# Attention stream of a trunk layer: layer norms written in four steps, the first output rows loaded one block sooner, the value products of a group in one run

## The chip, the core and the metric

The kernel runs on one core of a Trainium2 chip. The core has five engines with a queue of their own each, which run their instructions in the order of the queue: PE (TensorE, matrix products; PEld is its weight load), DVE (VectorE), ACT (ScalarE), POOL (GpSimd) and SP (SyncE, which here issues the DMA transfers). The metric is the time of one execution on the device in microseconds (us), the median of several runs.

## What is computed

One decoder layer on 2048 rows of 1024 numbers: stick-breaking attention with 12 heads of 64, cross-attention of 4 heads into 256 memory rows, an output projection, a layer norm, a squared-ReLU MLP of width 4096 and a second layer norm. The part around the change:

```python
def stick_breaking_attention(q, k, v):
    for blk in range(seq // SB_BLOCK):
        z = jnp.einsum('bhtd,bhsd->bhts', qb, kb).astype(jnp.float32) * scale
        strict = jnp.arange(t1)[None, :] < jnp.arange(t0, t1)[:, None]
        log_stay = jnp.where(strict, jax.nn.log_sigmoid(-z), 0.0)
        later = lax.cumsum(log_stay, axis=3, reverse=True) - log_stay
        w = jnp.where(strict, jnp.exp(jax.nn.log_sigmoid(z) + later), 0.0)
        outs.append(jnp.einsum('bhts,bhsd->bhtd', w.astype(vb.dtype), vb))
...
y = jnp.concatenate([mix, mem_out.astype(mix.dtype)], axis=-1) @ w_out[layer]
x = layer_norm(DN_ALPHA * x + y, ln_mix_g[layer], ln_mix_b[layer])
h = jnp.square(jax.nn.relu(x @ w_up[layer]))
x = layer_norm(DN_ALPHA * x + h @ w_down[layer], ln_ffn_g[layer], ln_ffn_b[layer])
```

## The kernel before

**Numbers.** Products run in fp16 with each operand split into a high and a low half, so a product is three passes (`PASSES`). ACT makes a high half, DVE or POOL the low one (`split_ps`, L161 and L162).

**Stages.** A first stage transposes x, projects the first pair of heads and does the memory heads (to about 236 us of the span). Then `attention` writes one long stream for the six pairs of heads p = 0 to 5 (240 steps, to about 1177 us), then comes a stretch in which the last output rows are projected and the operands of the MLP are transposed (to about 1255 us), then the MLP in two halves with the second layer norm (`finish`).

**The stream.** Rows go in four blocks c of 512, keys in blocks pc of 512. A step is one 128-row piece i of a block against one key block, for both heads of a pair; four steps (i = 0 to 3) are a group, so there are 60 groups. In step n the code writes, in this order: what is due (`later(k, fn)` puts fn k steps ahead), `score` of step n+1 (PE, z, L272, into four banks, two per step), `stay` (ACT, a sigmoid, L447), `scan` of step n (DVE, a running product and sum, e, L455), `spread` of step n-1 (ACT and POOL make the halves t, L309 and L310, and SP transposes them into w by DMA, L311; pieces of the diagonal that are short go through PE instead) and then a share of the fill work. `gather` (PE, av, L332) multiplies the transposed weights of a group with the values, 12 matmuls for each of its four key pieces `sblk`; all of them need the transposes of the last piece i = 3 of the group. `BEHIND` is how many steps after that transpose's step the products stand.

**Fill.** The segments name the work that is spread over the steps: projections of the next pair (24 matmuls a unit), and from the last two pairs on (a = 4, b = 5) the loads of w_out, and for the row tiles tb = 0 to 11 `out_proj_load` (mx from DRAM, acc from x) and two units of `out_proj` (op, L625, 24 matmuls each). Block 2 of pair a starts the first of these units.

**The layer norm of a row block.** After the last product of a tile, `add` (DVE, L632) and `stats` (DVE, L568), then for the four tiles of the block `norm` and, one step apart, `apply`: lnnb (DVE, L588), a scale on ACT (L589), two products with gamma on POOL (L592), two additions of beta on DVE (L593).

**What sets the order.** For the stream the order of each engine's queue is the order in which the code writes (each instruction is tied to the one ahead of it on its engine). After it, a scheduler places what is ready by priority.

Of the kernel before, what the change touches and what calls it, by code (L numbers as in the profile page):

```python
# [12 lines left out]
AF = mybir.ActivationFunctionType  # L13
ALU = mybir.AluOpType
# [3 lines left out]
C = 512  # L18
# [16 lines left out]
def trunk_layer(ctx: ExitStack, tc: tile.TileContext, x, mem, w_in, w_kv, w_out,  # L35
                g1, b1, w_up, w_down, g2, b2, out):
    nc = tc.nc
    V, A, G, T = nc.vector, nc.scalar, nc.gpsimd, nc.tensor
# [12 lines left out]
    NT = S // P  # L51
    NC = S // C
    TB = C // P
    NH = D // C
# [51 lines left out]
    def later(n, fn):  # L106
        if clock[0] is None:
            fn()
        else:
            due.setdefault(clock[0] + n, []).append(fn)  # L110
# [376 lines left out]


    FILL = (0.45, 0.45, 0.85, 1.1)
    BEHIND = 3  # L490

    def attention(segments, tail):

        first = nc.cur_bb.bb.instructions[-1] if nc.cur_bb.bb.instructions else None
        steps, starts = [], {}
        for blocks, done, units in segments:
            mine = [[Score(p, c, pc, h, i) for h in range(2)] for p, c in blocks for pc in range(c, -1, -1)
                    for i in range(TB)]  # L500
            starts[len(steps)] = units, [FILL[t.i] if t.diag else 1.0 for t, _ in mine], done
            steps += mine
        N = len(steps)
        work, spent, total = None, 0, 0
        for n in range(-1, N + BEHIND + 3):
            clock[0] = n
            if n in starts:
                if work is not None:
                    run(work)
                units, weight, done = starts[n]  # L510
                begin, spent, total, full = n, 0, sum(k for k, _ in units), sum(weight) * done
                work = (cost for _, u in units for cost in u())
            for fn in due.pop(n, []):
                fn()
            if n + 1 < N:
                score(steps[n + 1])
                stay(steps[n + 1])
            if 0 <= n < N:
                scan(steps[n])
            if 0 <= n - 1 < N:  # L520
                spread(steps[n - 1])
                t = steps[n - 1][0]
                if t.i == TB - 1:
                    for sblk in range(TB):
                        later(BEHIND + sblk // 2, lambda t=t, sblk=sblk: gather(t.p, t.c, t.pc, sblk))
            if work is not None:
                so_far = sum(weight[:n + 1 - begin]) if n < N else full
                while spent < total * min(1.0, so_far / full):
                    cost = next(work, None)
                    if cost is None:  # L530
                        spent = total
                        break
                    spent += cost
                if n >= N:
                    run(work)
            if n == N:
                tail()
        n += 1
        while due:
            clock[0] = n  # L540
            for fn in due.pop(n, []):
                fn()
            n += 1
        clock[0] = None
        ins = nc.cur_bb.bb.instructions
        last = {}
        on = first is None
        for i in ins:
            if on and i.engine in ENGINES:
                if i.engine in last:  # L550
                    tc.add_manual_dep(i, last[i.engine].name, ISSUE, reason="in order")
                last[i.engine] = i
            on = on or i is first


    gb = {}
# [26 lines left out]
        V.tensor_tensor(rs, rs, t, ALU.mult)  # L583
        return rs

    def ln_apply(r, mean, rstd, late):
        nb = sb.tile([P, 1], F32, name="lnnb", bufs=4)
        V.tensor_scalar(nb, mean, rstd, -1.0, ALU.mult, ALU.mult)  # L588
        A.activation(r, r, AF.Identity, bias=nb, scale=rstd)  # L589
        for n in range(NH):  # L590
            sl = r[:, n * C:(n + 1) * C]
            G.tensor_tensor(sl, sl, gb["g", n], ALU.mult)  # L592
            (G if late > n else V).tensor_tensor(sl, sl, gb["b", n], ALU.add)  # L593

    acc = {}
    x1 = dr.tile([NT, P, D], F32, name="x1")

    mixed = {}
    moments = {}
# [13 lines left out]
    def out_proj(tb, n):  # L613

        c, i = divmod(tb, TB)
# [31 lines left out]

        def apply(j, rs):
            t = c * TB + j
            ln_apply(acc[t], moments[c][:, j, 0:1], rs[:, j:j + 1], 0)  # L650
            if t >= NT // 2:
                nc.sync.dma_start(x1[t], acc[t])

        later(1, add)

# [353 lines left out]
    def kq(p, c):  # L1009
        return [unit(fn, p, c) for fn in (proj_k, proj_q)]  # L1010
# [11 lines left out]
    seq = []  # L1022
    for j, (load, u0, u1) in enumerate(flat):
        ahead = [flat[j + 1][0]] if j + 1 < len(flat) else []
        seq += ([load] if j == 0 else []) + ahead + [u0, u1]

    def take(n):
        got, out = 0, []
# [5 lines left out]
    def among(units, k):  # L1034
        return [u for j, unit in enumerate(units) for u in (unit, out_load(k + j))]
# [1 line left out]
    segments.append(([(a, 0)], 0.7, among(kq(a, 1), 0)))  # L1037
    segments.append(([(b, 0)], 0.7, among(kq(b, 1), 2)))
    segments.append(([(a, 1)], 0.8, among(kq(a, 2), 4)))
    segments.append(([(b, 1)], 0.8, among(kq(b, 2), 6)))  # L1040
    segments.append(([(a, 2)], 0.8, kq(a, 3) + take(4)))
    segments.append(([(b, 2)], 0.8, kq(b, 3) + [once(gamma)] + take(4)))
    segments.append(([(a, 3)], 1.0, take(8)))
# [92 lines left out]
```

## Time and profile before

| what | value |
|---|---|
| median of 3 runs | 2536.21 us (2528.76 to 2536.38) |
| profiled execution, its own time | 2532.38 us |
| span of its instructions | 2530.7 us |
| mean granted clock of PE | 0.962 |
| busy share PE / DVE / ACT / POOL | 91% / 68% / 47% / 41% |

The span runs from the first to the last instruction; 1.7 us of the execution lie around it. A busy share is a mean over stages with different limits. The granted clock is the share of full speed that PE was given.

### The profile page before, as it was taken

How to read it: one execution, taken by the hardware profiler on the slowest of the kernel's cores; microseconds unless marked ns; L12 is line 12 of the kernel's file. 1: busy time of each engine (PE TensorE's matmuls, PEld its weight loads, DVE VectorE, ACT ScalarE, POOL GpSimd, SP SyncE). 2: the span in 40 equal slices, each digit the busy share in tenths (PEclk: the TensorE clock that was granted, in tenths of full speed). 3: DMA queues.
4: the chain of work that ended last, by engine and by line, in shares of the span. 5: the costliest groups of instructions: out<-in, count | busy, mean ns of one | idle time of the engine just before them, and what ended most of it. 6: DMA issues, size and time to landing. Idle time of an engine off the chain costs nothing.

```text
span 2530.7 us, 34400 instructions
## 1 busy us (share of the span) xinstructions
PE 2291.2 (91%) x12032; PEld 1006.1 (40%) x12032; DVE 1713.4 (68%) x2385; ACT 1184.4 (47%) x2577; POOL 1038.8 (41%) x826
## 2 busy tenths in 40 slices
PE   7987999999899888789678999999999999999996
PEld 5433333333333333233333444444444444444443
DVE  4555777777676756666998888888767455555447
ACT  4555666666675644444454444544444222333321
POOL 0001555555564533545566544565327222111223
PEclk9998999999999989889899999999999999999998
DMA  7234778868786767467655433453365533233311
GB/s 254 42 81 82 145 153 141 154 124 156 141 159 134 142 142 162 103 131 183 175 193 177 143 117 133 159 182 132 104 207 180 174 99 100 86 106 100 100 42 67
DMA packets 606284, 342.02 MB, mean 135 GB/s; under 512 B 487840, under 2 KB 544672, under 8 KB 606112
## 3 DMA queue, kind: packets, MB, share of 16 engines
q1 hardware_dynamic: 606112, 339.84, 53.1%
q8 instruction: 94, 1.54, 0.3%
q14 instruction: 78, 0.64, 0.1%
HBM read 143.65 MB, written 77.59 MB: 87 GB/s over the span
## 4 chain that ended last, share of the span: by engine, by line
PE 53%; DVE 17%; issue 11%; DMA 7%; ACT 5%; POOL 5%; SPq 1%; POOLq 0%; DVEq 0%; ACTq 0%
PE dnb L862 7%; PE upb L786 7%; PE dnc L862 5%; PE dna L862 5%; DMA w<-t 4%; PE upc L786 4%; PE upa L786 4%; PE av L332 3%; POOL t L310 3%; DVE wr L670 3%; PE z L272 3%; PE op L625 3%; PE vp L252 3%; PE kp L252 2%; DVE e L455 2%
## 5 line engine op out<-in xcount | busy, mean ns | idle before, releaser
L310 POOL TENSOR_TENSOR t<-e,t 128x512 f16<-128x512 f32 (+1 forms) x384 | 434.7, 1154 | 482.8 <-ACT t L309 440.5
L877 POOL TENSOR_TENSOR acc<-acc,v 128x512 f32<-128x512 f32 x168 | 223.2, 1338 | 523.2 <-DVE acc L875 382.0
L786 PEld LDWEIGHTS <-rt 128*128 128x128 f16 x2688 | 266.6, 99 | 383.0 <-issue 69.4
L862 PEld LDWEIGHTS <-hl 128*128 128x128 f16 x2736 | 267.8, 98 | 334.4 <-issue 6.6
L447 ACT ACTIVATE z<-z 128x512 f32<-128x512 f32 (+1 forms) x480 | 226.4, 514 | 291.7 <-PE z L272 158.9
L455 DVE TENSOR_TENSOR_SCAN e<-z,carry,zero 128x512 f32<-128x512 f32 x288 | 347.7, 1262 | 21.0 <-ACT z L447 21.0
L786 PE MATMUL upb<-op,rt 128*128 128x512 f16 x1152 | 279.2, 393 | 43.9 <-DVE u L829 32.8
L862 PE MATMUL dnb<-wr,hl 128*128 128x512 f16 x1008 | 244.6, 379 | 0.2 <-DVE v L908 0.2
L272 PE MATMUL z<-k,q 64*128 64x512 f16 (+3 forms) x1440 | 196.6, 355 | 52.2 <-DVE e L455 46.6
L309 ACT ACTIVATE t<-e 128x512 f16<-128x512 f32 (+1 forms) x384 | 225.8, 616 | 11.4 <-DMA w<-t 11.2
L332 PE MATMUL av<-w,v 128*64 128x512 f16 (+3 forms) x1440 | 170.7, 357 | 36.4 <-DMA w<-t 35.3
L625 PE MATMUL op<-wo,mx 128*128 128x512 f16 x720 | 182.4, 404 | 12.3 <-DMA mx<-mix 9.5
L786 PE MATMUL upa<-op,rt 128*128 128x512 f16 x768 | 181.3, 382 | 7.4 <-DVE op L162 7.3
L786 PE MATMUL upc<-op,rt 128*128 128x512 f16 x768 | 178.4, 380 | 0.0
L862 PE MATMUL dnc<-wr,hl 128*128 128x512 f16 x672 | 168.1, 379 | 2.3 <-ACT hl L669 2.3
L862 PE MATMUL dna<-wr,hl 128*128 128x512 f16 x672 | 163.5, 379 | 4.9 <-DVE hl L797 3.2
L455 DVE TENSOR_TENSOR_SCAN e<-z,zero 128x128 f32<-128x128 f32 (+1 forms) x192 | 147.1, 806 | 21.5 <-ACT z L447 15.3
L252 PE MATMUL pq<-xT,wq 128*128 128x512 f16 x576 | 142.6, 389 | 8.2 <-DVE k L162 5.0
L252 PE MATMUL vp<-xT,wv 128*128 128x512 f16 x576 | 145.2, 395 | 1.0 <-ACT wv L143 1.0
L252 PE MATMUL kp<-xT,wk 128*128 128x512 f16 x576 | 140.7, 387 | 0.0
L792 ACT ACTIVATE u<-u 128x512 f32<-128x512 f32 x96 | 60.3, 629 | 161.9 <-DVE u L830 69.3
L895 ACT ACTIVATE v<-dna 128x512 f32<-128x512 f32 x56 | 32.4, 592 | 211.5 <-POOL acc L877 206.9
(176 smaller groups left out, 3226.2 us busy)
## 6 DMA issues: line engine op xcount, KB each, us to landing
keptdown<-wr SPq DMA_DIRECT2D x106, 256.0 KB, 3.4
wr<-keptdown SPq DMA_DIRECT2D x106, 256.0 KB, 3.0
keptup<-rt SPq DMA_DIRECT2D x48, 512.0 KB, 3.7
rt<-keptup SPq DMA_DIRECT2D x48, 512.0 KB, 3.5
wu<-in_w_up_dram SPq DMA_DIRECT2D x32, 512.0 KB, 4.5
wd<-in_w_down_dram SPq DMA_DIRECT2D x32, 512.0 KB, 4.1
x<-in_x_dram SPq DMA_DIRECT2D x16, 512.0 KB, 10.3
acc<-in_x_dram SPq DMA_DIRECT2D x16, 512.0 KB, 5.0
```

The costliest lines, as they stand in the source:

```text
L252: T.matmul(pp, lhsT=wt[:, a, k, :], rhs=xs(xT, c, b, k), start=n == 0, stop=n == 3 * KT - 1)
L272: T.matmul(banks[h], lhsT=q[rows, a, i * P:(i + 1) * P], rhs=keys(b)[rows], start=n == 0, stop=stop and n == 2)
L309: A.activation(hi, src, AF.Copy)
L310: G.tensor_tensor(lo, src, hi, ALU.subtract)
L332: T.matmul(av[h * HD:(h + 1) * HD, i0 * P:].rearrange("p (t n) -> p t n", n=P), lhsT=vv(h, a), rhs=pT(h, b)[:, i0:, :], start=first and n ...
L447: A.activation(t.z[:, :t.W], t.z[:, :t.W], AF.Sigmoid, scale=-SCORE)
L455: V.tensor_tensor_scan(t.e[:, t.W - 1::-1], t.z[:, t.W - 1::-1], zero[:, 0:1].broadcast_to([P, t.W]), init, ALU.mult, ALU.add)
L625: T.matmul(pp, lhsT=lhs, rhs=W[f"o{k}"][:, kb, n * C:(n + 1) * C], start=m == 0, stop=m == 3 * NKO - 1)
L670: V.scalar_tensor_tensor(lo, src, scale, hi, ALU.mult, ALU.subtract)
L786: T.matmul(bv, lhsT=r[:, a, k, :], rhs=operand(ops, s, b, k), start=start and n == 0, stop=n == 3 * HB - 1, skip_group_check=not start)
L862: mm = T.matmul(bank, lhsT=hl[s][:, g, a, i * P:(i + 1) * P], rhs=wr[r][:, g, b, :], start=start and m == 0, stop=m == 3 * n - 1, skip_gro ...
L877: G.tensor_tensor(sl, sl, u, ALU.add)
```

## The change

Three things are written differently. `ln_apply` no longer writes its four parts (lnnb, scale, products, additions) into one step of the stream: each stands one step after the one before; outside the stream nothing is put off, and the parts follow each other at once. The first `out_proj_load` moves from the start of block 2 of pair a to the start of block 1 of pair b. The four value products of a group stand together, four steps after the last transpose, where two stood three steps and two four steps after it. The store of a normalised tile to x1 follows its additions.

```diff
-    BEHIND = 3
+    BEHIND = 4
...
                     for sblk in range(TB):
-                        later(BEHIND + sblk // 2, lambda t=t, sblk=sblk: gather(t.p, t.c, t.pc, sblk))
+                        later(BEHIND, lambda t=t, sblk=sblk: gather(t.p, t.c, t.pc, sblk))
...
-    def ln_apply(r, mean, rstd, late):
+    def ln_apply(r, mean, rstd, late, then=None):
         nb = sb.tile([P, 1], F32, name="lnnb", bufs=4)
         V.tensor_scalar(nb, mean, rstd, -1.0, ALU.mult, ALU.mult)
-        A.activation(r, r, AF.Identity, bias=nb, scale=rstd)
-        for n in range(NH):
-            sl = r[:, n * C:(n + 1) * C]
-            G.tensor_tensor(sl, sl, gb["g", n], ALU.mult)
-            (G if late > n else V).tensor_tensor(sl, sl, gb["b", n], ALU.add)
+
+        def scale():
+            A.activation(r, r, AF.Identity, bias=nb, scale=rstd)
+            later(1, gains)
+
+        def gains():
+            for n in range(NH):
+                sl = r[:, n * C:(n + 1) * C]
+                G.tensor_tensor(sl, sl, gb["g", n], ALU.mult)
+            later(1, shifts)
+
+        def shifts():
+            for n in range(NH):
+                sl = r[:, n * C:(n + 1) * C]
+                (G if late > n else V).tensor_tensor(sl, sl, gb["b", n], ALU.add)
+            if then is not None:
+                then()
+
+        later(1, scale)
...
         def apply(j, rs):
             t = c * TB + j
-            ln_apply(acc[t], moments[c][:, j, 0:1], rs[:, j:j + 1], 0)
-            if t >= NT // 2:
-                nc.sync.dma_start(x1[t], acc[t])
+            keep_rows = (lambda: nc.sync.dma_start(x1[t], acc[t])) if t >= NT // 2 else None
+            ln_apply(acc[t], moments[c][:, j, 0:1], rs[:, j:j + 1], 0, keep_rows)
...
-        seq += ([load] if j == 0 else []) + ahead + [u0, u1]
+        seq += ahead + [u0, u1]
...
-    segments.append(([(b, 1)], 0.8, among(kq(b, 2), 6)))
+    segments.append(([(b, 1)], 0.8, [flat[0][0]] + among(kq(b, 2), 6)))
```

What moves in the queues is shown at three places. In the names the digits after a letter are the pair, then block c, key block pc, piece i and head; the last number is a buffer.

DVE, the layer norm of row block 0 while pair 4 goes through its block 3 (acc0 and acc1 are the first two of the four tiles). Before:

```order
L455 SCALAR_TENSOR_TENSOR e4_3_3_3_1_10965<-z4_3_3_3_1_10893,zero_76 128x512
L588 TENSOR_SCALAR lnnb_11004<-mv_10106,lnrs_10942 128x1
L593 TENSOR_TENSOR acc0_9917<-acc0_9917,gb1_0_10474 128x512
L593 TENSOR_TENSOR acc0_9917<-acc0_9917,gb1_1_10475 128x512
L632 SCALAR_TENSOR_TENSOR acc4_10591<-acc4_10591,op4_0_10846 128x512
L455 SCALAR_TENSOR_TENSOR e4_3_2_0_0_11022<-z4_3_2_0_0_10953,carry_10870,zero_76 128x512
L455 SCALAR_TENSOR_TENSOR e4_3_2_0_1_11024<-z4_3_2_0_1_10954,carry_10870,zero_76 128x512
L588 TENSOR_SCALAR lnnb_11054<-mv_10106,lnrs_10942 128x1
L593 TENSOR_TENSOR acc1_9921<-acc1_9921,gb1_0_10474 128x512
L593 TENSOR_TENSOR acc1_9921<-acc1_9921,gb1_1_10475 128x512
```

And in the changed kernel, from the last lnnb of the block on (L603 is the addition, L646 the `add`):

```order
L588 TENSOR_SCALAR lnnb_11146<-mv_10106,lnrs_10930 128x1
L603 TENSOR_TENSOR acc0_9416<-acc0_9416,gb1_0_10474 128x512
L603 TENSOR_TENSOR acc0_9416<-acc0_9416,gb1_1_10475 128x512
L646 SCALAR_TENSOR_TENSOR acc5_10796<-acc5_10796,op5_0_11046 128x512
L455 SCALAR_TENSOR_TENSOR e4_3_2_3_0_11165<-z4_3_2_3_0_11108,carry_10870,zero_76 128x512
L455 SCALAR_TENSOR_TENSOR e4_3_2_3_1_11167<-z4_3_2_3_1_11109,carry_10870,zero_76 128x512
L603 TENSOR_TENSOR acc1_9921<-acc1_9921,gb1_0_10474 128x512
L603 TENSOR_TENSOR acc1_9921<-acc1_9921,gb1_1_10475 128x512
```

The additions of a tile stood right behind its lnnb; now three scans' steps lie between the two, and the four pairs of additions stand ahead of the scans of four steps that held none before.

SP, the first output rows (mx0, acc0). Before, at the start of block 2 of pair 4:

```order
L311 DMA_TRANSPOSE w4_2_2_0_9760<-t4_2_2_3_0_9905 128x8x128
L311 DMA_TRANSPOSE w4_2_2_1_9761<-t4_2_2_3_1_9910 128x8x128
L608 DMA mx0_9915<-mix0_78 128x2048
L611 DMA acc0_9917<-in_x_dram 128x1024
L608 DMA mx1_9919<-mix0_78 128x2048
```

In the changed kernel, at the start of block 1 of pair 5:

```order
L311 DMA_TRANSPOSE w4_1_0_0_9287<-t4_1_0_3_0_9406 128x8x128
L311 DMA_TRANSPOSE w4_1_0_1_9288<-t4_1_0_3_1_9410 128x8x128
L622 DMA mx0_9414<-mix0_78 128x2048
L625 DMA acc0_9416<-in_x_dram 128x1024
L311 DMA_TRANSPOSE w5_1_1_0_9442<-t5_1_1_2_0_9507 128x6x128
L311 DMA_TRANSPOSE w5_1_1_1_9443<-t5_1_1_2_1_9512 128x6x128
```

The two transfers stand about 20 rows further up; the load of the second tile (mx1) keeps its place.

PE, the values of pair 1, block 1, key block 0. Before, the first half-run stands between a projection of the fill (kp2) and the scores of the next group's first piece (z1_2_1_0):

```order
L252 LDWEIGHTS wk2_3459
L252 MATMUL kp2_0_4338<-xT00_0_158,wk2_3459 128x512
L332 LDWEIGHTS v1_0_2162
L332 MATMUL av1_1_4180<-w1_1_0_0_4125,v1_0_2162 64x512
L332 LDWEIGHTS v1_0_2162
L332 MATMUL av1_1_4180<-w1_1_0_1_4126,v1_0_2162 64x512
```

In the changed kernel the scores follow the projection at once:

```order
L252 LDWEIGHTS wk2_3459
L252 MATMUL kp2_0_4338<-xT00_0_158,wk2_3459 128x512
L272 LDWEIGHTS q1_2_3330
L272 MATMUL z1_2_1_0_0_4350<-k1_0_2700,q1_2_3330 128x512
L272 LDWEIGHTS q1_2_3330
L272 MATMUL z1_2_1_0_1_4351<-k1_0_2700,q1_2_3330 128x512
```

The first 24 value products of the group move down to stand with the other 24, ahead of the scores of one step later.

## Rows read from the trace of the kernel before

**Rows 1.** The page, first part: busy time, share of the span, instructions.

```profile
PE 2291.2 (91%) x12032; PEld 1006.1 (40%) x12032; DVE 1713.4 (68%) x2385; ACT 1184.4 (47%) x2577; POOL 1038.8 (41%) x826
```

**Rows 2.** Windows by stage: stretch, length, busy time of each engine, clock, DMA.

```profile
236.50:783.10 546.60, 500.18 (x3189) 200.40 (x3191) 398.24 (x446) 367.81 (x944) 319.14 (x286) 0.99 0.79 146
...
942.90:996.60 53.70, 50.83 (x306) 21.05 (x302) 34.06 (x42) 26.00 (x68) 23.28 (x22) 0.97 0.79 165
996.60:1088.80 92.20, 74.12 (x381) 27.92 (x378) 61.58 (x77) 40.91 (x96) 46.60 (x38) 0.89 0.61 128
1088.80:1177.50 88.70, 78.14 (x407) 30.10 (x406) 62.91 (x77) 42.13 (x98) 43.73 (x36) 0.90 0.57 127
1177.50:1255.30 77.80, 56.30 (x290) 28.75 (x286) 61.99 (x90) 28.69 (x48) 39.95 (x30) 0.91 0.78 203
```

**Rows 3.** Waits of PE, 236.5 to 783.1 us: us in total, times, longest.

```profile
PE av L332 <- DMA w<-t: 22.5, 30, 1.4
PE z L272 <- DVE e L455: 19.3, 29, 3.1
```

**Rows 4.** Waits of PE, 783.1 to 1177.5 us.

```profile
PE av L332 <- DMA w<-t: 12.4, 9, 4.9
PE op L625 <- DMA mx<-mix: 9.5, 1, 9.5
```

**Rows 5.** Timeline at the first output product: start, length, instruction [idle before].

```profile
905.93 0.53 SPq L608 DMA_DIRECT2D mx<-mix  x1
...
909.80 5.83 PE L625 MATMUL op<-wo,mx 128*128 128x512 f16 x16 [9.52 <-DMA mx<-mix]
...
916.32 3.84 PE L625 MATMUL op<-wo,mx 128*128 128x512 f16 x17
```

**Rows 6.** Timeline of one step of the first layer norm, 1026 to 1036 us.

```profile
1026.65 1.24 ACT L589 ACTIVATE acc<-acc,lnnb,lnrs 128x1024 f32<-128x1024 f32 x1 [4.71 <-DVE lnnb L588]
...
1027.97 2.49 POOL L592 TENSOR_TENSOR acc<-acc,gb 128x512 f32<-128x512 f32 x2 [3.41 <-ACT acc L589]
...
1029.27 3.29 DVE L593 TENSOR_TENSOR acc<-acc,gb 128x512 f32<-128x512 f32 x2 [2.65 <-POOL acc L592]
...
1035.01 0.39 PE L272 MATMUL z<-k,q 64*128 64x512 f16 x1 [3.07 <-DVE e L455]
```

**Rows 7.** Windows of one step of each of the two layer norms.

```profile
1024.10:1033.70 9.60, 6.35 (x21) 1.93 (x20) 6.95 (x9) 3.46 (x7) 6.07 (x5) 0.82 0.65 174
...
1113.70:1123.40 9.70, 7.36 (x20) 2.28 (x20) 7.05 (x9) 3.46 (x7) 6.75 (x5) 0.65 0.65 172
```

**Rows 8.** Instructions of L593 in the whole span, ns: least, median, most.

```profile
L593 DVE TENSOR_TENSOR acc<-acc,gb x38: 668/1645/1757, 1020.2 to 2520.9; 128x512 f32<-128x512 f32 x38
```

**Rows 9.** Groups by form on DVE, 996.6 to 1088.8 us: busy, mean ns | idle before.

```profile
L455 DVE TENSOR_TENSOR_SCAN e<-z,carry,zero 128x512 f32<-128x512 f32 x25 | 30.4, 1259 | 1.5 <-ACT z L447 1.5
L593 DVE TENSOR_TENSOR acc<-acc,gb 128x512 f32<-128x512 f32 x8 | 13.2, 1688 | 18.7 <-POOL acc L592 18.7
L632 DVE SCALAR_TENSOR_TENSOR acc<-acc,op 128x512 f32<-128x512 f32 x8 | 5.4, 678 | 6.0 <-PE op L625 5.9
L568 DVE BATCH_NORM_STATS2 lnst<-acc 128x6 f32<-128x512 f32 x8 | 5.0, 672 | 0.0
```

**Rows 10.** Timeline of PE around one group's value products, 409 to 420 us.

```profile
411.10 1.46 PE L332 MATMUL av<-w,v 128*64 128x512 f16 x11 [0.95 <-DMA w<-t]
...
415.29 1.49 PE L332 MATMUL av<-w,v 128*64 128x512 f16 x12
416.71 0.82 PE L272 MATMUL z<-k,q 64*128 64x512 f16 x6
...
419.51 0.82 PE L272 MATMUL z<-k,q 64*128 64x512 f16 x6
```

**Rows 11.** Waits of PE, 1177.5 to 1260 us.

```profile
PE op L625 <- DVE m L297: 8.5, 1, 8.5
PE upa L786 <- DVE op L162: 7.3, 1, 7.3
```

## The prediction

> **What bounds the kernel now.** I read the page first. PE is busy for 91% of the span, DVE for 68% [rows 1], so time can only be won where PE waits or runs at a lower clock, and the page doesn't say where. The windows by stage do [rows 2]. The long even part of the stream (236.5 to 783.1) has PE busy for 500.2 of 546.6 us, 46 us idle. The stretch 942.9 to 996.6, twelve steps with output products in the fill and no layer norm, is nearly full: 50.8 of 53.7. The two stretches behind it do the same kind of work with a layer norm in it, and are worse in two ways: PE idles 18.1 of 92.2 and 10.6 of 88.7 us, and the granted clock is 0.89 and 0.90. The reader is to see there that the cost of a wait is larger than the idle time beside it.
>
> Then the waits of PE, by stretch. In the even part two kinds matter: value products that wait for the transposed weights (22.5 us in 30 waits, none over 1.4) and scores that wait until DVE's scan has freed a bank (19.3 in 29) [rows 3]. Later there is one wait of 9.5 us for mx, and 12.4 us more for transposes, of which one wait is 4.9 [rows 4].
>
> **First load.** The timeline has mx0 issued by SP at 905.93, PE standing idle for 9.52 us until it lands, and then 16 output products in 5.83 us, where 17 a little later take 3.84 [rows 5]. The load stands on SP behind transposes, and its first user on PE comes one piece of fill after it. Moved a block up, it has some 50 us. The idle time goes, and with it the slow start: 16 x 3.84 / 17 = 3.6, so 5.83 - 3.6 = 2.2. Sum **11.7 us**. The two transfers are now issued between other transposes (0.53 us for mx0); no value product needs those for three steps, so I cost that at nothing; without this cover it would be about 1 us. What is late next could be mx1, which keeps its place, but its user comes two units later. Lower bound 6, if DVE's scans, which stood still in the same gap, are late by half of it.
>
> **The layer norm in four steps.** No instruction is added or removed. In a step of the norm [rows 6] ACT's scale starts at 1026.65, POOL's products at 1027.97, DVE's additions at 1029.27, after 2.65 us of waiting for POOL, and they end at 1032.56. DVE's queue is in order, so the scans behind them wait, the scores wait for the scans (3.07 us idle), and one step takes 9.6 to 9.7 us [rows 7]. In the new order the additions find the scale written two steps and the products one step ahead of them, so this wait goes (18.7 us on DVE in the first block [rows 9]); what remains is DVE's work.
>
> What would the stretch then take? The yardstick is 942.9 to 996.6: 50.8 us of PE work for 12 steps and six units. The stretch of the first norm has 16 steps and eight units: two units more are 2 x 24 x 3.84 / 17 = 10.8, four steps' scores 4 x 0.82 and one group's values about 2.9 [rows 10], together 50.8 + 10.8 + 3.3 + 2.9 = 68 us at full clock. In four of the steps DVE needs more than PE. DVE: two scans 2.5, two additions 3.4, and as shares of a step about 0.4 for `add`, 0.4 for the statistics, 0.2 for lnnb: 6.9 us [rows 9]. PE: scores 0.82, 13 output products 2.9, a quarter of a group's values 0.7: 4.5. Four times 2.4 is 9.6; PE can be one step's scans ahead in its four banks, which takes off 2.5. So 7 us of waiting, and 1.5 for small waits: 76.5 to 77. **First norm: 92.2 - 77 = 15. Second: 2 us of first transposes for the MLP come on top, 88.7 - 79 = 10.** Bounds: an addition takes 0.67 alone and 1.65 as the median [rows 8], since POOL works beside it; at 0.67 DVE's step is 4.9, all but 1 us is absorbed, and the gains are 22 and 17. The other end is the clock, below: 7 and 1.5.
>
> The additions will now meet POOL's work of other steps more often, so I keep the longer duration. A rule of the Trainium skill speaks against this part: SBUF — State Buffer, section "SBUF: two separate sides", says that VectorE with two SBUF inputs and GpSimd take a shared port pair in turn, and that the loser waits for the whole instruction of the other. The median of 1.65 beside the 0.67 agrees. By that rule an addition could wait for all of a POOL product before it (half of 2.49 us [rows 6]), 1.25 + 0.67 = 1.9 in place of 1.69, and each norm would gain some 2 us less.
>
> **Value products in one run.** 60 groups. The first half-run of a group waits for the transposes (0.95 us in the middle of it [rows 10]), the second, one step later, does not. Standing a light step later (2.8 us from one set of scores to the next, 416.71 to 419.51), and behind no half-run, both find their data: the longest of the 30 waits was 1.4. So 22.5 us and, of the 12.4, all but the 4.9 that lies in the first norm's stretch: 7.5, together 30 us can go. Not all of it will be kept. PE has three light steps in a row now, and in these it needs 2.8 us and DVE 2.5 for its scans, 3.2 when a projection's low half comes on top, so the scores will wait for a scan a little oftener. DVE is busy for 398 of 546.6 us, so on the whole there is room. I keep two thirds: **20 us**. Bounds 0 and 30; a loss is the third rival.
>
> **Behind the stream.** 1177.5 to 1255.3 is DVE's: 62.0 of 77.8 us, with PE waiting 8.5 us for a low half and 7.3 for the last transposed operand [rows 11]. The low half moves up in DVE's queue, past additions that were ahead of it, but these come behind it and delay the operands. DVE's sum is the same. **2 us**, from 4 lost to 8 won. In the MLP the same instructions stand in a slightly other order: nothing, give or take 3.
>
> **Sum.** 11.7 + 15 + 10 + 20 + 2 = 58.7. The profiled execution took 2532.4 us of its own, 3.8 below the median of the three runs and inside their spread. 2532.4 - 58.7 = 2473.7, so **2474 us**.
>
> **Rivals.**
> The waits for transposes only turn into waits for scans. For it: the two kinds are of one size now [rows 3], and PE's light steps are as long as DVE's. Against it: DVE idles 27% of that stretch. The 20 us are lost: 2494.
>
> The clock stays low in the norms. In a step of the norm now, PE works for 6.35 of 9.6 us and 7.36 of 9.7 and the granted clock is 0.82 and 0.65 [rows 7]; in 942.9 to 996.6, where it waits less, 0.97 [rows 2]. If PE, waiting for DVE 2.4 us in each of the four steps, still ran at half its speed, such a step would need 9.0 on PE in place of 6.9: 4 x 2.1 = 8.4 us a norm, so gains of 7 and 1.5: 2491. The levels are 1.2 and 2.4 GHz. TensorE: Matmul & The Clock Gate, section "HAM oscillation — how this bites in real kernels", tells of a loop whose products run at the lower level because a wait comes back in every round; the two clocks above agree, and by that rule the 2491 would be the result. I think it less likely, since 2.4 us of 6.9 is a smaller part than what is idle now once the slow products are counted at full speed (9.6 less about 5).
>
> The other side: the run of 24 value products stands ahead of the next scores, so a scan starts 1.49 us later [rows 10] in each of 60 groups. Where PE is the limit this costs nothing; if DVE were, it would cost up to 60 x 1.49 = 89 us: 2494 + 89 = 2583. It ends above the old time from 0.65 us a group on (38.7 / 60). Against it: DVE's idle share again.
>
> The first load doesn't free PE, because mx1 or the last rows of w_out are late in its place: 11.7 less, 2485.
>
> **How the numbers follow.** Forecast 0.62, waits turned into scan waits 0.20, low clock 0.10, late first load 0.04, starved scans 0.04. The likeliest case by itself spans 2460 to 2488. The range takes in the first three rivals that are no loss and the bounds of the additions: 2458 to 2500. Under 0.3% (7.6 us) this kernel can't be told from no change; all cases but the slow one end below that, and I leave something for several going wrong together: faster 0.93, same 0.03, slower 0.04.
>
> **What would show it.** Right: no wait of PE for mx near 900 us of the span; steps of the two norms at about 7 us with no DVE wait for POOL ahead of the additions, the stretches at about 77 and 79 us; waits of value products for transposes under 5 us in the whole stream, with those of scores for scans at most 10 us up. Wrong: scan waits up by as much as the others fell; a clock under 0.8 in the norm's steps; additions that still wait for POOL.

## The result, and the profile after

The changed kernel takes 2459.05 us (median of 5 runs, 2456.57 to 2465.01), the kernel before in the same session 2536.38 us (5 runs): ratio 0.9703, interval 0.9687 to 0.9719, so 77 us faster. The forecast was 2474, its range 2458 to 2500. The profiled execution took 2465.0 us, 6 above its median; 67.4 us less than the profiled one of before.

(One count ahead of the prediction is wrong: a key piece has 6 value products and a group 24, so a half-run is 12, as the prediction says.)

The page, first part, which answers to [rows 1]:

```profile
PE 2265.9 (92%) x12032; PEld 1006.3 (41%) x12032; DVE 1702.5 (69%) x2385; ACT 1182.8 (48%) x2577; POOL 1034.2 (42%) x826
```

The same instructions, but PE is busy for 25 us less. Windows by stage, cut at the same places of the program as [rows 2] (stretch, length, busy time of PE, PEld, DVE, ACT, POOL, clock, DMA share, GB/s):

```profile
238.20:764.70 526.50, 488.13 (x3184) 200.01 (x3186) 396.55 (x446) 367.91 (x946) 317.26 (x286) 0.99 0.83 151
...
858.80:907.80 49.00, 48.83 (x302) 20.85 (x302) 33.69 (x40) 26.95 (x69) 22.29 (x21) 1.00 0.86 165
907.80:956.50 48.70, 48.70 (x305) 20.76 (x304) 33.94 (x42) 25.93 (x68) 23.28 (x22) 1.00 0.88 181
956.50:1028.50 72.00, 65.93 (x367) 26.78 (x366) 60.03 (x77) 40.76 (x96) 46.29 (x38) 0.95 0.75 157
1028.50:1104.80 76.30, 72.28 (x419) 29.67 (x418) 59.33 (x77) 42.06 (x98) 42.76 (x37) 0.98 0.74 153
1104.80:1179.10 74.30, 56.59 (x291) 28.62 (x286) 56.97 (x89) 27.63 (x45) 35.38 (x26) 0.91 0.77 186
1179.10:2463.30 1284.20, 1206.80 (x5488) 543.02 (x5487) 876.10 (x1251) 479.25 (x823) 497.26 (x349) 0.97 0.40 131
```

Read beside [rows 2]: the even stretch is 20.1 us shorter (546.6 to 526.5), the one with the first output products 16.5 (65.5 to 49.0), the next 5.0, the two norms 20.2 and 12.4. The stretch behind the stream is 3.5 shorter, and the MLP 8.8 longer (1275.4 us before). The window of the first output products in the kernel before, which [rows 2] leave out, is this:

```profile
877.40:942.90 65.50, 53.43 (x304) 21.46 (x302) 33.52 (x40) 27.81 (x71) 23.39 (x22) 0.90 0.64 139
```

The waits of PE in the even stretch, and from there to the end of the stream, answer to [rows 3, 4] (us in total, times, longest):

```profile
PE z L272 <- DVE e L455: 29.5, 42, 3.1
...
PE av L332 <- DMA w<-t: 1.8, 4, 0.7
...
PE z L272 <- DVE e L455: 16.0, 20, 2.4
...
PE av L332 <- DMA w<-t: 2.5, 3, 1.2
```

The wait for mx is gone. In the even stretch 20.7 us of waits for transposes went and 10.2 us of waits for scans came. The timeline of PE at the first output product, against [rows 5], has no idle time and 16 products in 3.63 us, where they took 5.83:

```profile
876.26 0.82 PE L272 MATMUL z<-k,q 64*128 64x512 f16 x6
877.02 3.63 PE L639 MATMUL op<-wo,mx 128*128 128x512 f16 x16
```

The timeline in the first norm, against [rows 6] (all engines, so the rows overlap):

```profile
982.11 1.23 ACT L591 ACTIVATE acc<-acc,lnnb,lnrs 128x1024 f32<-128x1024 f32 x1
...
985.05 2.50 POOL L597 TENSOR_TENSOR acc<-acc,gb 128x512 f32<-128x512 f32 x2
...
986.36 3.31 DVE L603 TENSOR_TENSOR acc<-acc,gb 128x512 f32<-128x512 f32 x2 [0.59 <-POOL acc L597]
...
987.51 3.18 POOL L310 TENSOR_TENSOR t<-e,t 128x512 f16<-128x512 f32 x2
...
989.59 0.67 DVE L646 SCALAR_TENSOR_TENSOR acc<-acc,op 128x512 f32<-128x512 f32 x1
```

DVE's wait for POOL ahead of the additions fell from 2.65 us to 0.59 in this step; over the block it is 0.6 in place of the 18.7 of [rows 9]:

```profile
L603 DVE TENSOR_TENSOR acc<-acc,gb 128x512 f32<-128x512 f32 x8 | 12.0, 1534 | 0.6 <-POOL acc L597 0.6
```

Windows of three steps, from scan to scan, against the 9.6 and 9.7 of [rows 7]:

```profile
983.25:990.19 6.94, 6.94 (x38) 2.71 (x36) 6.35 (x8) 6.90 (x16) 6.88 (x6) 1.00 0.85 223
990.19:995.18 4.99, 4.50 (x39) 2.19 (x38) 4.99 (x6) 2.34 (x6) 4.99 (x5) 1.00 0.72 158
995.18:1001.35 6.17, 5.27 (x25) 1.97 (x24) 6.17 (x6) 2.76 (x8) 6.17 (x5) 1.00 0.45 86
```

In the second and third DVE is busy all the time, PE waits a little, and the clock stays at 1.00.

### The profile page after: what moved, and what is told of

Read it like the earlier page. It is cut to its first block, busy times and chain, and to the rows that moved or that the text cites. A ratio compares the mean times of both kernels' runs of the same rounds, so it can differ in the third digit from the quotient of the medians.

```text
span 2463.3 us, 34394 instructions
## 1 busy us (share of the span) xinstructions
PE 2265.9 (92%) x12032; PEld 1006.3 (41%) x12032; DVE 1702.5 (69%) x2385; ACT 1182.8 (48%) x2577; POOL 1034.2 (42%) x826
## 4 chain that ended last, share of the span: by engine, by line
PE 45%; DVE 13%; DMA 3%; issue 3%; ACT 2%; POOL 2%; SPq 0%; DVEq 0%; POOLq 0%; ACTq 0%
PE upb L799 8%; PE dnb L875 8%; PE dnc L875 6%; PE dna L875 5%; PE upc L799 4%; PE upa L799 4%; PE op L639 4%; DVE wr L683 2%; PE dn L875 2%; DVE rt L683 2%; DVE acc L603 1%; DVE e L455 1%; PE z L272 1%; PE av L332 1%; DMA wd<-in_w_down_dram 1%
## 5 line engine op out<-in xcount | busy, mean ns | idle before, releaser
L309 ACT ACTIVATE t<-e 128x512 f16<-128x512 f32 (+1 forms) x384 | 226.4, 616 | 13.2 <-DMA w<-t 12.2
L799 PE MATMUL upa<-op,rt 128*128 128x512 f16 x768 | 185.4, 388 | 14.9 <-ACT u L832 10.7
L639 PE MATMUL op<-wo,mx 128*128 128x512 f16 x720 | 172.2, 388 | 1.2 <-DVE acc L646 1.2
L455 DVE TENSOR_TENSOR_SCAN e<-z,zero 128x128 f32<-128x128 f32 (+1 forms) x192 | 147.0, 805 | 22.7 <-ACT z L447 16.5
L332 PE MATMUL av<-w,v 128*64 128x512 f16 (+3 forms) x1440 | 148.9, 352 | 7.1 <-DMA w<-t 5.9
L908 ACT ACTIVATE v<-dna 128x512 f32<-128x512 f32 x56 | 32.4, 592 | 214.9 <-POOL acc L890 210.3
```

The source lines that it names most:

```text
L309: A.activation(hi, src, AF.Copy)
L332: T.matmul(av[h * HD:(h + 1) * HD, i0 * P:].rearrange("p (t n) -> p t n", n=P), lhsT=vv(h, a), rhs=pT(h, b)[:, i0:, :], start=first and n ...
L455: V.tensor_tensor_scan(t.e[:, t.W - 1::-1], t.z[:, t.W - 1::-1], zero[:, 0:1].broadcast_to([P, t.W]), init, ALU.mult, ALU.add)
L639: T.matmul(pp, lhsT=lhs, rhs=W[f"o{k}"][:, kb, n * C:(n + 1) * C], start=m == 0, stop=m == 3 * NKO - 1)
L799: T.matmul(bv, lhsT=r[:, a, k, :], rhs=operand(ops, s, b, k), start=start and n == 0, stop=n == 3 * HB - 1, skip_group_check=not start)
```

## The experiments

For each run the stretches below are cut at the first scan of a segment, in its profiled execution, so each row is one execution; the last column reaches to the end of the span. "Pairs 0 to 3" is the even stretch with the first block of pair 0. Columns 4/2 and 5/2 are block 2 of pairs 4 and 5, 4/3 and 5/3 the two with a norm.

| kernel | prologue | pairs 0 to 3 | pairs 4, 5, blocks 0, 1 | 4/2 | 5/2 | 4/3 | 5/3 | behind |
|---|---|---|---|---|---|---|---|---|
| before | 210.3 | 572.8 | 94.3 | 65.5 | 53.7 | 92.2 | 88.8 | 1353.1 |
| changed | 210.4 | 554.4 | 94.1 | 49.0 | 48.7 | 72.0 | 76.3 | 1358.5 |
| norm alone | 208.1 | 573.1 | 96.4 | 65.1 | 53.4 | 75.7 | 77.8 | 1354.4 |
| load alone | 211.4 | 572.1 | 94.1 | 52.7 | 53.4 | 92.1 | 89.2 | 1353.8 |
| values alone, one run | 209.5 | 552.7 | 93.6 | 59.6 | 48.7 | 79.1 | 87.1 | 1361.9 |
| values alone, halves | 209.8 | 543.9 | 90.4 | 60.9 | 50.4 | 82.2 | 89.3 | 1361.1 |
| changed, halves | 209.9 | 542.7 | 90.9 | 49.6 | 50.4 | 70.8 | 75.9 | 1355.0 |
| one run, three behind | 211.6 | 586.2 | 91.5 | 64.1 | 53.5 | 93.3 | 92.2 | 1363.9 |
| changed, halves in pairs 0 to 3 | 211.2 | 542.5 | 92.9 | 48.8 | 48.7 | 72.0 | 77.7 | 1353.1 |
| norm in two steps | 208.5 | 575.1 | 94.6 | 63.0 | 55.2 | 74.6 | 72.7 | 1355.2 |
| changed, additions on POOL | 211.6 | 550.9 | 93.9 | 49.0 | 48.7 | 69.3 | 72.1 | 1356.9 |
| changed, four operations on DVE | 208.9 | 551.3 | 93.8 | 48.9 | 48.7 | 74.0 | 77.7 | 1353.0 |
| changed, halves and POOL | 208.1 | 542.0 | 91.1 | 49.5 | 50.4 | 68.8 | 70.0 | 1365.0 |

The part behind the stream, whose code is nearly the same in all, takes from 1353.0 to 1365.0 us in these single executions: a difference of a few us in that column is no finding.

The kernel before ran beside the experiments at 2534.9, 2534.6 and 2534.6 us.

**1. The norm alone.** The `ln_apply` in four steps and the later store, on the kernel before.

```diff
-        A.activation(r, r, AF.Identity, bias=nb, scale=rstd)
-        for n in range(NH):
...
+        later(1, scale)
```

> The kernel before with the layer norm in four steps alone. My theory: the parts of the change add up, and this one is the largest. In the changed kernel's trace the two stretches with a norm are 20.2 and 12.5 us shorter, 32.7 together, of which some 3 to 5 us belong to the value products that no longer wait in them; the start of the MLP gives some 5 us back. So 22 to 30 us faster than before, with the first stretch at 73 to 77 us and PE's wait for mx (9.5 us) still there. Terms as predicted: 15 + 10 + 2 = 27. Rival: the granted clock only came back because the other waits went as well; then this part alone gives 8.5 us (7 and 1.5), and the clock in the norm's steps stays under 0.85.

Measured 2505.9 us, ratio 0.9882 (0.9863 to 0.9900): 29.0 us. Windows of the two stretches:

```profile
996.20:1071.90 75.70, 67.05 (x381) 26.52 (x378) 60.22 (x77) 40.75 (x96) 46.51 (x38) 0.95 0.75 154
1071.90:1149.70 77.80, 72.09 (x407) 29.15 (x407) 59.59 (x77) 42.01 (x98) 42.67 (x36) 0.98 0.69 146
```

16.5 and 11.0 us shorter, with the clock at 0.95 and 0.98 where [rows 2] have 0.89 and 0.90, and the wait for mx still there (9.7 us). The rival of a clock that needs the other parts to recover falls.

**2. The first load alone.**

```diff
-        seq += ([load] if j == 0 else []) + ahead + [u0, u1]
+        seq += ahead + [u0, u1]
...
+    segments.append(([(b, 1)], 0.8, [flat[0][0]] + among(kq(b, 2), 6)))
```

> The kernel before with the first output rows loaded one block sooner, and nothing else. My theory: 11.7 us, the idle 9.5 and the slow start of 2.2; the stretch in which the first output products stand is 53 to 54 us in place of 65.5. The changed kernel shows 49.0 there, 16.5 less, so up to 16.5 if the slow clock ahead of the gap (0.92 from 877.4 to 900) comes back with it as well. Rival: the next load or the scans behind it take the place of the wait, 0 to 6 us.

Measured 2519.9 us, ratio 0.9939 (0.9922 to 0.9955): 14.9 us; the stretch is 52.7 us, 12.8 shorter, and no other column of the table moves by more than 1.1. Nothing took the place of the wait. The window of the stretch:

```profile
877.72:930.42 52.70, 49.81 (x302) 20.68 (x301) 33.50 (x41) 27.78 (x71) 23.38 (x22) 1.00 0.81 154
```

**3. The values alone, in one run.**

```diff
-    BEHIND = 3
+    BEHIND = 4
...
-                        later(BEHIND + sblk // 2, lambda t=t, sblk=sblk: gather(t.p, t.c, t.pc, sblk))
+                        later(BEHIND, lambda t=t, sblk=sblk: gather(t.p, t.c, t.pc, sblk))
```

> The kernel before with the value products of a group in one run, four steps behind, and nothing else. My theory: 20 us, from waits for transposes that go (22.5 us in the even stretch, and some 7 later) less scan waits that grow by 10; the even stretch, 546.6 us before, falls to about 527, as it does with all three parts. Other reading of the same trace: half of the gain isn't waiting at all, since PE's busy time in that stretch fell by 12 us and its idle time by 8; it comes with the run, so it is seen here too. Rival: without the shorter norms the runs of 24 starve the scans in the last two pairs, and the whole gives under 12.

Measured 2494.1 us, ratio 0.9839 (0.9818 to 0.9861): 40.8 us, twice the theory. The even part of it is as expected (20.1 us over pairs 0 to 3). The rest came in columns 4/2, 5/2 and 4/3: 5.9, 5.0 and 13.1 us, with 8.8 lost behind the stream in this execution. The rival of starved scans falls.

**4. The values alone, a step later but in halves.**

```diff
-    BEHIND = 3
+    BEHIND = 4
```

> The kernel before with the value products one step later but still in two halves: two key pieces four steps behind, two five steps. Theory A: what costs is the wait for transposes, and standing a step later cures it; then this is as fast as the one run, within 4 us, and PE's busy time in the even stretch falls to about 488 as there. Theory B: PE's busy time fell because a run of 24 changes half as often from one kind of product to another (0.1 us or more at each of 60 changes fewer, and as many scans held up as before); then this is 4 to 14 us slower than the one run, with the waits for transposes gone all the same and PE busy for 494 to 500 us.

Measured 2491.5 us, ratio 0.9827 (0.9808 to 0.9845): no slower than the one run, and not to be told from it. Windows over pairs 0 to 3, one fence each for before, one run and halves:

```profile
210.30:783.10 572.80, 518.17 (x3279) 207.48 (x3279) 410.65 (x468) 378.25 (x973) 320.59 (x287) 0.98 0.77 143
```

```profile
209.50:762.20 552.70, 505.69 (x3274) 206.97 (x3274) 409.11 (x469) 378.39 (x975) 318.67 (x287) 0.98 0.81 148
```

```profile
209.80:753.70 543.90, 506.41 (x3277) 202.69 (x3275) 409.44 (x469) 378.72 (x976) 319.65 (x287) 0.99 0.83 150
```

PE's busy time falls by 12 us in both, so it does not take the single run to save it: it goes with the waits. Experiment 5, a single run that keeps the waits, saves none. Theory B, as it was put, falls. It does not follow that merging saves nothing: the value products by themselves (L332) are busy for 113.5 us over these pairs before, 96.6 in one run and 103.9 in halves. What the one run gains there it gives back on other lines of PE; that was not taken apart. What differs is PE's idle time, 572.8 - 518.2 = 54.6 before, 47.0 with one run and 37.5 with halves. In the waits of the halves (237.0 to 753.7 us) scores wait 24.5 us for scans, with one run (236 to 761) 30.2; the waits of pt (the short diagonal pieces that PE transposes) for DVE differ by nearly as much, 2.8 against 7.9:

```profile
PE z L272 <- DVE e L455: 24.5, 36, 3.1
PE pt L319 <- DVE w L162: 2.8, 11, 0.3
PE av L332 <- DMA w<-t: 1.9, 3, 1.2
```

```profile
PE z L272 <- DVE e L455: 30.2, 42, 3.1
PE pt L319 <- DVE w L162: 7.9, 11, 1.6
...
PE av L332 <- DMA w<-t: 0.9, 3, 0.4
```

So the run of 24 has a price after all, in waits for DVE of both kinds: 8.8 us over 40 groups, 0.22 us a group. The timeline of PE with halves shows the value products spread, with scores between them, where one run is 2.78 us without a score:

```profile
405.19 1.49 PE L332 MATMUL av<-w,v 128*64 128x512 f16 x12
406.61 0.82 PE L272 MATMUL z<-k,q 64*128 64x512 f16 x6
407.37 2.12 PE L252 MATMUL kp<-xT,wk 128*128 128x512 f16 x9
409.41 1.49 PE L332 MATMUL av<-w,v 128*64 128x512 f16 x12
```

**5. One run, three steps behind** (on the kernel before).

```diff
     BEHIND = 3
...
-                        later(BEHIND + sblk // 2, lambda t=t, sblk=sblk: gather(t.p, t.c, t.pc, sblk))
+                        later(BEHIND, lambda t=t, sblk=sblk: gather(t.p, t.c, t.pc, sblk))
```

> The kernel before with the value products of a group in one run, but three steps behind, so that the second half moves up to the first and nothing moves down. Theory A (the gain of the values came from standing a step later, not from the run): the waits for transposes stay at 20 us or more in the even stretch, PE's busy time there stays near 500, and the whole is within 4 us of the kernel before or up to 10 slower, since the runs hold scans up. Theory B (the run gives the gain): 10 us or more faster than before.

Measured 2552.9 us, ratio 1.0072 (1.0055 to 1.0089): 18 us slower, further than theory A had it. The window of pairs 0 to 3, and the waits of PE in it:

```profile
211.60:797.80 586.20, 521.15 (x3293) 215.36 (x3291) 409.73 (x468) 377.37 (x974) 320.71 (x287) 0.97 0.74 140
```

```profile
PE z L272 <- DVE e L455: 28.9, 40, 3.1
PE av L332 <- DMA w<-t: 20.8, 25, 2.6
```

The waits for transposes stay, those for scans are added to them, and PE is busy for 521.2 us, no less than the 518.2 before: standing a step later is what gains, the run is what loses.

**6 and 7. The changed kernel with halves again.** In all pairs, or in pairs 0 to 3 only:

```diff
-                        later(BEHIND, lambda t=t, sblk=sblk: gather(t.p, t.c, t.pc, sblk))
+                        later(BEHIND + sblk // 2, lambda t=t, sblk=sblk: gather(t.p, t.c, t.pc, sblk))
```

```diff
-                        later(BEHIND, lambda t=t, sblk=sblk: gather(t.p, t.c, t.pc, sblk))
+                        later(BEHIND + (sblk // 2 if t.p < NP - 2 else 0), lambda t=t, sblk=sblk: gather(t.p, t.c, t.pc, sblk))
```

> The changed kernel, but with the value products in two halves again, four and five steps behind. Alone on the kernel before the halves gave 43.3 us and the run 40.8; by stretch the halves were 8.8 us shorter over pairs 0 to 3 (543.9 against 552.7 us) and 5 to 9 us longer in the last four stretches and behind the stream. Theory A: the run of 24 holds the next scores up and so the scan, which costs in the even stretch, and the halves lose it again where the norm's additions stand; then this is about 2455 (4 us faster than the changed kernel). Theory B: the later loss came from the unsplit norm; with the norm in steps only the gain is left: 2450. Rival: no difference beyond 2 us, 2459.

> The changed kernel with halves (four and five steps behind) for pairs 0 to 3 and the run of 24 for pairs 4 and 5. Theory A (a run of 24 costs 0.24 us a group in the even stretch through the scans that it holds up): pairs 0 to 3 take about 544 us in place of 552 to 554, all later stretches as in the changed kernel: 2450 to 2451. Rival (the shorter even stretch of the halves only came from another place of a fill unit, and is gone here): 2457 to 2461.

Measured 2446.7 us, ratio 0.9646 (0.9628 to 0.9663), and 2445.5 us, ratio 0.9642 (0.9625 to 0.9659): both 12 to 14 us below the changed kernel, with intervals that lie wholly under its own. Pairs 0 to 3 take 542.7 and 542.5 us in place of 554.4. This does not hang on one execution: the four kernels with the run of 24 four steps behind take 550.9 to 554.4 us there, the four with halves 542.0 to 543.9. In the later columns halves in all pairs cost nothing on balance now: 5/2 is 1.7 us longer than in the changed kernel and 4/3 is 1.2 shorter, 70.8 us with PE at a clock of 1.00.

```profile
943.30:1014.10 70.80, 63.95 (x376) 26.07 (x376) 60.74 (x76) 40.74 (x96) 46.23 (x38) 1.00 0.81 166
```

Theory B of the first, and theory A of the second; both gained more than expected.

**8. The norm in two steps** (on the kernel before: lnnb, scale and products together, additions one step later; the diff is against the four steps of 1).

```diff
             A.activation(r, r, AF.Identity, bias=nb, scale=rstd)
-            later(1, gains)
+            gains()
...
-        later(1, scale)
+        scale()
```

> The kernel before with the norm in two steps in place of four: lnnb, scale and products in one step, the additions one step later. Theory A (only DVE's wait for POOL ahead of the additions cost, and scale and products take 3.7 us, less than a step): as fast as the four steps, 2502 to 2510. Rival (POOL, waiting in order for the scale, is late with the low halves of the weights, so that transposes and value products are late): 5 to 15 us slower than the four steps, with more waits for transposes in the two norm stretches than there (5.3 and about 2).

Measured 2501.9 us, ratio 0.9869 (0.9853 to 0.9884), not to be told from the four steps. Value products wait 4.9 us for transposes in the two norm stretches, 6.1 with four steps, so the rival falls. Of the three distances only the one between POOL's products and DVE's additions shows in the time.

**9. The additions on POOL** (changed kernel).

```diff
-            ln_apply(acc[t], moments[c][:, j, 0:1], rs[:, j:j + 1], 0, keep_rows)
+            ln_apply(acc[t], moments[c][:, j, 0:1], rs[:, j:j + 1], 2, keep_rows)
```

> The changed kernel with the two additions of beta of each tile of the norm of row blocks 0 to 2 on POOL in place of DVE. Theory A (as in the prediction: what is left in the norm's steps is DVE's own work, 3.3 us of additions of some 6): the waits of scores for scans in the two norm stretches (4.1 and 4.0 us) go for the most part, the stretches are 2 to 4 us shorter each, and behind the stream DVE, which is busy for 57 of 74 us there, gives 2 to 4 more: 2449 to 2455. Theory B (POOL is then late with the low halves of the weights, since it carries 5 us a tile where the step has 5): waits for transposes come up by as much or more: 2459 to 2468.

Measured 2455.9 us, ratio 0.9682 (0.9666 to 0.9699), 3 us below the changed kernel's median and just above theory A's span, with intervals that overlap. In the windows the two norm stretches are 2.6 and 4.2 us shorter, PE is almost full (65.1 of 69.4, 70.1 of 72.1) and DVE has room: this fits the reading that DVE's own work is what remains there. But scores still wait 4.1 us for scans in the two, where they waited 8.0: half of it went and not most, and of the 6.8 us by stretch only 3 stand in the medians.

```profile
954.10:1023.50 69.40, 65.11 (x373) 26.97 (x372) 48.42 (x69) 42.74 (x97) 53.25 (x47) 0.98 0.73 151
1023.50:1095.60 72.10, 70.13 (x413) 29.76 (x412) 50.39 (x70) 40.95 (x95) 49.71 (x44) 0.98 0.80 172
```

**10. The application as four operations on DVE** (changed kernel).

```diff
...
+            V.scalar_tensor_tensor(sl, sl, mean, gb["g", n], ALU.subtract, ALU.mult)
+            V.scalar_tensor_tensor(sl, sl, rstd, gb["b", n], ALU.mult, ALU.add)
...
```

> The changed kernel with the norm's application of row blocks 0 to 2 as two operations on DVE for each half of a tile: (r - mean) x gamma, then x rstd + beta, and nothing on ACT or POOL, so no wait between engines. DVE has four such operations per tile in place of two additions. Theory A (an addition takes 1.65 us only while POOL's product of the norm runs beside it; alone 0.67): four take 2.7 us, less than the 3.3 of now, and each norm stretch is 0 to 3 us shorter: 2453 to 2459. Theory B (POOL's other work, the low halves t, stretches DVE's operations as well): four take up to 6.6 us, 3.3 more in each of 8 steps, up to 26 longer: 2470 to 2485.

Measured 2456.7 us, ratio 0.9681 (0.9662 to 0.9700): the time is within theory A's span, the mechanism lies between the two. The instructions of the first of these lines (ns: least, median, most):

```profile
L612 DVE SCALAR_TENSOR_TENSOR acc<-acc,mv,gb x32: 721/744/1855, 964.3 to 1184.6; 128x512 f32<-128x512 f32 x32
```

The median is 0.74 us, but 11 of the 32 operations in the two norm stretches took over 1 us, beside POOL's other work, as this one beside a low half t:

```profile
965.73 1.36 POOL L310 TENSOR_TENSOR t<-e,t 128x384 f16<-128x384 f32 x1
966.24 1.40 DVE L612 SCALAR_TENSOR_TENSOR acc<-acc,mv,gb 128x512 f32<-128x512 f32 x1
```

So theory B has part of it. Four operations take 4.2 us a tile in the first norm and 3.6 in the second, where A has 2.7 and B 6.6; the two additions of the changed kernel take 3.0 and 2.4. DVE has more work than before, and the norm stretches, 74.0 and 77.7 us, are 2.0 and 1.4 longer than in the changed kernel. What the median gains all the same comes from no stretch that was taken apart, and the intervals overlap.

**11. Halves and additions on POOL together** (changed kernel with the edits of 6 and 9).

```diff
+                        later(BEHIND + sblk // 2, lambda t=t, sblk=sblk: gather(t.p, t.c, t.pc, sblk))
...
+            ln_apply(acc[t], moments[c][:, j, 0:1], rs[:, j:j + 1], 2, keep_rows)
```

> The changed kernel with both edits that helped: value products in halves four and five steps behind, and the norm's additions on POOL. If they add: 2446.7 - 3.2 = 2443.5, so 2440 to 2447, faster than every kernel so far. Rival: the halves have already filled what the additions on POOL win (the norm stretches are 70.8 and 75.9 there), or POOL is late with the low halves now that products stand nearer to the transposes of the next group: 2446 to 2452.

Measured 2444.5 us, ratio 0.9642 (0.9626 to 0.9657): as expected by addition, but not to be told from the halves alone, so the 2 us are left open. The two norm stretches are 2.0 and 5.9 us shorter than with halves alone, but in these executions the part behind the stream is 10.0 longer. It is the lowest median of all.

## Why the prediction was right, point by point

The time was inside the range at its lower end; the direction and the mechanisms held, and one term was mis-sized by half.

**First load: 11.7 predicted, 14.9 measured alone** (12.8 in its stretch). Right, a little short: with the gap gone the clock of the stretch was 1.00 where it had been 0.90, and PE's busy time in it fell by 3.6 us (53.4 to 49.8), while the sum had taken only the 2.2 of the one slow run of 5.83 us behind the gap. The load stood 37 us ahead of its first product (840.0 against 877.0 in the changed kernel), not some 50, and that was enough.

**Norms: 15 + 10 and 2 behind the stream, 27 predicted, 29.0 measured alone** (16.5 and 11.0 in the two stretches). The yardstick of the full stretch held: 68 us of PE's work were expected in the first norm, 67.1 were measured with the norm alone, and the stretches took 75.7 and 77.8 us for the 77 and 79. DVE's work per step was put a little high: 6.4, 5.0 and 6.2 us in the windows of three steps above for the 6.9. The low-clock rival did not come. TensorE: Matmul & The Clock Gate, section "HAM oscillation — how this bites in real kernels", of the Trainium skill tells of a loop in which the work of a round "is shorter than the DMA-wait". The steps of the norm are not such a loop: in the windows above PE works for 4.5 of 5.0 us and 5.3 of 6.2, and the clock is 1.00. One window of the second norm of the changed kernel does show the lower level in part of it, so the rival was not baseless:

```profile
1063.00:1069.00 6.00, 5.62 (x21) 1.93 (x23) 6.00 (x7) 3.43 (x7) 5.62 (x5) 0.72 0.52 101
```

The 2 us behind the stream were not there: alone, the norm takes 4.1 us off the stretch behind the stream and adds 4.8 to the next, from the first up product to the first product into dnb (47.3 to 52.1). That this is because the additions then still stand in DVE's queue is my reading; with the additions on POOL (experiment 9) the same stretch is 42.3 us where the changed kernel has 53.5, which fits, but what follows it is as much longer. DVE's sum is the same, as the prediction said, and the stretch was cut in the wrong place to see it.

**Values: 20 predicted, bounds 0 to 30; 40.8 measured alone.** This is the term that failed. The step was "So 22.5 us and, of the 12.4, all but the 4.9 that lies in the first norm's stretch: 7.5, together 30 us can go". It counted idle time alone. Over pairs 0 to 3 the deduction for scan waits was too small (of 21.6 us of waits for transposes that went, 10.9 came back as scan waits, half and not a third), but PE's busy time fell by 12.5 us as well: in the group of [rows 10] the first value product follows a wait and stands alone for 0.38 us, and the other 11 take 1.46, where 12 in a run take 1.49. This is the row of that first product:

```profile
409.77 0.38 PE L332 MATMUL av<-w,v 128*64 128x512 f16 x1 [0.55 <-DMA w<-t]
```

In pairs 0 to 3 of the kernel before, 21 of the 80 half-runs are split like this; at 0.35 us each that is some 7 of the 12.5 us, an estimate, and the rest was not taken apart. The prediction's first paragraph had said that a wait costs more than the idle time beside it; this should have gone into the sum. The stretches 4/2, 5/2 and 4/3 then gave 24 us where 7.5 had been allowed in all: 5/2 went from 50.8 to 48.7 us busy and from 0.97 to 1.00 in clock as its 2.9 us of waits went. How the 13.1 of 4/3 divide between the waits, the clock and the other order of DVE's work was not taken apart.

**The rival "waits turn into scan waits"** came true by half in the even stretch, and what PE's busy time lost outweighed it. **The rival on the other side** (runs starve the scans) exists at 0.22 us a group, a third of the 0.65 from which it decides; experiments 4 to 7 show it, and the fastest kernels are those that avoid it.

**The sum.** The parts alone give 29.0 + 14.9 + 40.8 = 84.7, the whole 77.3. They meet in 4/3, where the norm alone takes off 16.5 and the values alone 13.1, both together 20.2, and in 4/2, where the load alone takes off 12.8 and the values alone 5.9, all together 16.5: one idle stretch can be filled once. Of this the prediction had left out only one wait of 4.9, and it hid part of the short term. So by luck 58.7 came nearer to 77 than the terms deserved. (The executions of the changed kernel and of the values alone are 5 to 9 us longer than before behind the stream, but two other kernels with later values have 1353.1 and 1353.0 there, as before, so this is not put down to the values.)

**The additions.** The duration that was kept (1.65) is still the median over the whole span: 665/1642/1779 ns against [rows 8]. In the two norms the eight additions take 12.0 and 9.7 us, where each eight took 13.2 before.

## What to carry to other kernels

Price a wait of the bounding engine at its idle time plus the slow restart and the lower clock behind it; here 21.6 us of waits removed also took 12.5 us of "busy" time away. When an in-order engine waits for a transfer, move the work later, but do not bunch it: a step later in two halves beat a step later in one run by 12 us in the changed kernel (by nothing clear in the kernel before, where later stretches lost it again), and one run without the step lost 18. When several edits fill the same idle stretch, sum them by stretch, with what is idle there as the cap.

## What the runs showed of the hardware

An addition with both operands in SBUF does not run slower beside POOL, it waits for POOL's instruction to end, and the wait is counted in its recorded duration. Rows of DVE and POOL in the second norm:

```profile
1069.69 1.71 POOL L597 TENSOR_TENSOR acc<-acc,gb 128x512 f32<-128x512 f32 x1
1070.20 1.75 DVE L603 TENSOR_TENSOR acc<-acc,gb 128x512 f32<-128x512 f32 x1
```

```profile
1078.64 2.26 POOL L310 TENSOR_TENSOR t<-e,t 128x512 f16<-128x512 f32 x2
1081.23 1.27 DVE L603 TENSOR_TENSOR acc<-acc,gb 128x512 f32<-128x512 f32 x2
1083.69 1.16 POOL L310 TENSOR_TENSOR t<-e,t 128x512 f16<-128x512 f32 x1 [2.79 <-ACT t L309]
```

The addition at 1070.20 starts while POOL is at work, which ends at 1071.40, and ends at 1071.95, 0.55 us later. The pair at 1081.23 begins when POOL is done (1078.64 + 2.26 = 1080.90) and takes 1.27 us, 0.67 and 0.69. In the two norms of the changed kernel 14 of the 16 additions start beside a POOL instruction, and all 14 end 0.55 us after it, whether it is a product of the norm or a low half; so do the 11 longer operations of experiment 10. POOL waits in the same way: its product at 1069.69 started while the addition before was under way and took 1.71 us, where the median is 1.28. The `add` of an output product, one of whose operands is in PSUM, ran at 989.59 for its 0.67 us in the middle of POOL's pair from 987.51 to 990.69, and none of the 32 took more than 0.69. SBUF — State Buffer, section "SBUF: two separate sides", of the Trainium skill says that the loser waits for the whole instruction; the rows agree. The prediction's bound by that rule was 1.9 us an addition; the longest was 1.78 and the mean in the first norm 1.53 (12.0 us for 8), so the 2 us a norm that it would have cost were not lost.
